# Second gate of the linear attention as a third seven-product block product, with two weight sums of each left to accumulating transfers

## The chip, the core and the metric

The kernel runs on one core of a Trainium2 chip. The time is device microseconds of one execution, the median of several; the profile is one more execution with the hardware profiler on. Engines are named as in the profile: PE is TensorE (PEld its weight loads), DVE is VectorE, ACT is ScalarE, POOL is GpSimd, SP is SyncE, which here only issues transfers.

## What is computed

One transformer block on 512 tokens of width 1024, in float32. A single weight `w_in` gives all projections of the normed input; two branches run from them, a gated linear attention in both directions with 4 heads and a latent attention with 8 heads; they are merged through two sigmoid gates, and a squared-ReLU network follows. What matters here, cut from the reference:

```python
n = rmsnorm(h, g_mix[l])
proj = n @ w_in[l]
(gq, gk, gv, gr, z_gf, z_gb, cq, ckv, kr, z_ma, z_mb) = jnp.split(proj, SPLIT_IDX, axis=-1)
...
o = rmsnorm(o_f + o_b, g_gla.reshape(GLA_HEADS, GLA_DV))
o = o.reshape(B, S, GLA_V_W) * jax.nn.silu(gr.astype(jnp.float32))     # y_gla
...
merged = jax.nn.sigmoid(z_ma) * y_gla + jax.nn.sigmoid(z_mb) * y_mla
h = h + merged @ w_out[l]
```

So the linear attention's output has two gates of the same width of 1024: the inner one, `gr`, and the outer one, `z_ma` (called za in the kernel). `z_mb` (zb) gates the latent attention.

## The kernel before, in words

**Precision.** Each float32 operand is split in a high part (rounded by a ScalarE copy, line 93) and a low part (the rest, by VectorE, line 94). `mm3` (lines 88 to 90) multiplies with three matmuls: high by high, high by low, low by high.

**Chunks.** A projection chunk is 128 columns of `w_in` against all 512 tokens: the weight (128x1024) is loaded by SP into one of 3 staging buffers, split into one of 4 pairs of weight buffers, and multiplied in 24 matmuls of 128x512 (`proj_begin`, `proj_run`). The result has features on partitions and tokens along the row. gq, gk, zb, za and the latents cq and ckv are done in such chunks. In za's case `za_gate` then multiplies by the row factor R on VectorE, takes tanh and a scale with bias (the gain of the norm) on ScalarE.

**Seven products.** gr and gv (1024 columns each) are done by class `Seven` as a 2 by 2 block product with seven multiplications instead of eight, after Winograd. Left factors are quarters of the input and four sums of them (`x_sums`, POOL); right factors are four weight blocks and four sums of them, made on VectorE (`less`, `right_sums`, line 608) in the place of a block. The order is 1, 2, 5, 6, 3, 7, 4. Each product is 24 matmuls of 128x512, and the results have tokens on partitions. Results of several products are added in six buffers c11, c12, c22 by ScalarE copies (line 660) and VectorE additions (line 663); a product that accumulates on an accumulator that was copied must wait for the copy. The sums and splits of a product are prepared two products ahead. Chunks are put between products as fillers: zb4, the small gate chunk, gq1, gk1 and, last, zb5.

**The heads.** For head h = 0 to 2 a loop gives PE, in this order: the scores (`gla_scores`: bd, then sc0 to sc3, with copies of bd on ScalarE and masked copies and splits on VectorE), the two gate matmuls of head h+1 (`Gates`), za chunk 2h, the output of head h (`gla_out`, 48 matmuls of 128x256), za chunk 2h+1, gq and gk of head h+2 (for head 2: ckv0, ckv1), and the eight transposes y of the gated output (`gla_turn`). Beside it run, for head h+1: logarithm, scans and exponentials of the gates (lines 442 to 479), the products q and k by decay on VectorE (`gla_qk`, line 489) and eight more on POOL (line 497); and for head h: squares on ScalarE, the norm on POOL (lines 717 to 719) and the gated rows on VectorE (`gla_gated`, line 727). POOL works in order, so the norm of head h stands behind the eight products of head h+1. After the transposes VectorE multiplies by the za gate (line 741).

**Head 3 and the step to the attention.** After the loop come cq0 to cq2, zb6, the scores of head 3, za6, the scaling of the query latent (cqrs), za7, the first part of zb7, the rotary query (ro, from the scaled and split latent cqhl), the rest of zb7, the first up-projections (uq0, uk0), the output of head 3, the values (uv), and then the first scores (s) of the latent attention. Chunks uq1 and uk1 come between its first scores. Calls of `goes_behind` and marks fix parts of that order on PE.

**What sets the order.** The program is written as one Python function under a tile scheduler, which places instructions on in-order queues, one per engine, and sets all waits. `in_program_order` fixes the written order for PE from the first product to the end of the heads, for ScalarE and VectorE from the start to the end of the heads, and for POOL through the block products; the rest the scheduler may order by its own costs. Tiles come from pools with a fixed number of buffers: 26 of 128x1024 (u4), 29 of 128x512 (u2), 4 and 4 PSUM banks (tags at and mm), and a tile whose pool is full waits until the last reader of an older one is done.

Of the kernel before, what the change touches and what calls it, by code (L numbers as in the profile page):

```python
# [18 lines left out]
P = 128  # L19
# [37 lines left out]
def tile_block(ctx: ExitStack, tc: tile.TileContext, t, out: bass.AP):  # L57
# [496 lines left out]

    SEVEN = (1, 2, 5, 6, 3, 7, 4)
# [35 lines left out]
    class Seven:  # L591
# [3 lines left out]

        def load(self, x):

            self.blocks[x] = [u4(f"{self.name}w{x}{g}", F32, (P, 2, S)) for g in range(2)]
            for g in range(2):
                r = ((x // 2) * 4 + 2 * g) * P  # L600
                c = self.col + (x % 2) * S
                nc.sync.dma_start(
                    self.blocks[x][g], w_in[r : r + 2 * P, c : c + S].rearrange("(k p) w -> p k w", p=P)
                )

        def less(self, dst, x, y):
            for g in range(2):
                nc.vector.tensor_tensor(
                    self.blocks[dst][g], self.blocks[x][g], self.blocks[y][g], op=ALU.subtract
                )  # L610
# [12 lines left out]
        def right_split(self, m, g):  # L623
            x = {1: 0, 2: 2, 5: 0, 6: 0, 3: 3, 7: 1, 4: 2}[m]
# [14 lines left out]
        def multiply(self, m):  # L639
# [18 lines left out]
            if m in (1, 5, 6):  # L658
                for acc, c in zip(accs, {1: self.c11, 5: self.c22, 6: self.c12}[m]):
                    nc.scalar.activation(c, acc, AF.Copy)  # L660
            elif m in (2, 3, 7):
                for acc, c in zip(accs, {2: self.c11, 3: self.c12, 7: self.c22}[m]):
                    nc.vector.tensor_tensor(c, acc, c, op=ALU.add)
# [22 lines left out]
    za_gates, held = {}, {}  # L686
# [42 lines left out]
    def gla_turn(h, early=None):  # L729
# [3 lines left out]
        for dv in range(2):  # L733
# [6 lines left out]
            y = za_gates.pop(f)  # L740
            nc.vector.tensor_tensor(y, tp, y, op=ALU.mult)
# [337 lines left out]
    sevens = [Seven(C_GR, "gr", gr_rows), Seven(C_GV, "gv", gv_rows)]  # L1079
# [6 lines left out]

    def begin_za(f):
# [581 lines left out]
```

## Time and profile before

| | |
|---|---|
| median of 3 runs | 763.39 us (763.17 to 763.4) |
| the profiled execution | 762.79 us |
| its span, first to last instruction | 761.0 us |
| mean granted clock of TensorE | 0.999 |
| DVE busy | 580.7 us, 76% of the span |
| ACT busy | 453.3 us, 60% |
| POOL busy | 150.5 us, 20% |

Line numbers such as L608 are those of the kernel before. A row of the timeline has start and length in us, engine, line, operation, output and inputs, the shape, how many instructions were merged (x2), and in brackets the idle time ahead of it with what ended that. A row of groups has the total busy time and the mean of one in ns. A row of transfers has the size of one and the median from issue to landing.

### The profile page before, as it was taken

The numbers are of one execution on the slowest core, as the hardware profiler recorded it, in microseconds if no ns is written. First come the engines' busy times: TensorE is split into PE (matmuls) and PEld (weight loads), VectorE is DVE, ScalarE is ACT, GpSimd is POOL, SyncE is SP. The second block draws the span as 40 slices with busy tenths as digits, with TensorE's granted clock in tenths as the row PEclk, the third lists the DMA queues.
The fourth block names the chain that finished last, engine by engine and source line by source line (L and its number), as shares of the span: only waits on it lengthen the run. The fifth ranks groups of instructions, "written<-read, shape, count | busy, mean of one in ns | idle before, by whom it ended". The sixth has DMA issues, their size and how long they took to land.

```text
span 761.0 us, 10233 instructions
## 1 busy us (share of the span) xinstructions
PE 752.1 (99%) x3744; PEld 636.1 (84%) x3744; DVE 580.7 (76%) x850; ACT 453.3 (60%) x768; POOL 150.5 (20%) x226
## 2 busy tenths in 40 slices
PE   9999999999999999999999999999999999999996
PEld 7888788888898889898888988888888888888885
DVE  7779999756767775998897786955796578748795
ACT  8456668475466555888866675435553555345644
POOL 0710005260615104127761100000000000000014
PEclk9999999999999999999999999999999999999999
DMA  9843310221324416127988421362116410650002
GB/s 312 255 112 108 93 28 28 56 59 54 84 60 112 82 33 155 25 71 191 272 189 229 140 80 56 111 196 80 55 56 195 137 42 15 195 165 1 28 1 110
DMA packets 97185, 81.28 MB, mean 107 GB/s; under 512 B 15504, under 2 KB 74896, under 8 KB 97136
## 3 DMA queue, kind: packets, MB, share of 16 engines
q1 hardware_dynamic: 93904, 74.33, 33.3%
q0 software_dynamic: 2944, 6.03, 4.3%
q8 instruction: 29, 0.48, 0.3%
q10 hardware_dynamic: 288, 0.28, 0.1%
q14 instruction: 20, 0.16, 0.1%
HBM read 76.96 MB, written 2.10 MB: 104 GB/s over the span
## 4 chain that ended last, share of the span: by engine, by line
PE 97%; DVE 1%; ACT 1%; issue 0%; POOL 0%; POOLq 0%; ACTq 0%
PE f L88 8%; PE f L89 8%; PE f L90 8%; PE gx L88 4%; PE gx L90 4%; PE gx L89 4%; PE first L327 3%; PE tp L1042 2%; PE za L88 2%; PE za L89 2%; PE za L90 2%; PE gz L88 2%; PE gz L90 2%; PE gz L89 2%; PE zb L88 1%; PE zb L90 1%
## 5 line engine op out<-in xcount | busy, mean ns | idle before, releaser
L1608 POOL DMA_DIRECT2D gfin<-in_g_final x1 | 0.6, 622 | 284.0 <-PE f L90 284.0
L914 DVE TENSOR_TENSOR w<-w,w 128x1024 f32<-128x1024 f32 x32 | 38.7, 1221 | 0.3
L475 POOL COPY v3f<-rrf 128x4 f32<-128x4 f32 x4 | 2.8, 708 | 135.9 <-DVE rrf L458 135.9
L1027 ACT ACTIVATE e<-s,top 128x512 f32<-128x512 f32 x32 | 21.9, 685 | 4.8 <-DVE top L1022 3.9
L94 DVE TENSOR_TENSOR pT<-tp,pT 128x512 fp32r<-128x512 f32 x32 | 21.7, 682 | 2.9 <-ACT pT L93 2.9
L1022 DVE TENSOR_REDUCE top<-s 128x1 f32<-128x512 f32 x32 | 21.6, 681 | 2.0 <-PE s L90 1.7
L1335 DVE TENSOR_TENSOR h<-h,gx 128x512 f32<-128x512 f32 x32 | 21.5, 682 | 1.9 <-PE gx L90 1.8
L93 ACT ACTIVATE pT<-tp 128x512 fp32r<-128x512 f32 x32 | 18.8, 593 | 4.2 <-PE tp L1042 3.9
L1042 PE MATMUL tp<-ident,e 128*128 128x128 f32 x128 | 19.3, 274 | 0.4 <-ACT e L1033 0.2
L88 PE MATMUL av<-pT,v 128*128 128x256 f32 x64 | 19.0, 297 | 0.0
L93 ACT ACTIVATE ghb<-y 128x512 fp32r<-128x512 f32 x16 | 10.1, 632 | 14.0 <-DVE y L860 14.0
L1401 ACT ACTIVATE fa<-f 128x512 f32<-128x512 f32 x32 | 18.5, 577 | 0.0
L89 PE MATMUL av<-pT,v 128*128 128x256 f32 x64 | 18.2, 285 | 0.0
L1042 PEld LDWEIGHTS tp<-ident,e 128*128 128x128 f32 x128 | 15.1, 140 | 3.7 <-ACT e L1033 1.0
L94 DVE TENSOR_TENSOR sc<-sc,sc 128x512 fp32r<-128x512 f32 x16 | 10.9, 691 | 9.5 <-ACT sc L93 9.5
L90 PE MATMUL av<-pT,v 128*128 128x256 f32 x64 | 18.1, 283 | 0.0
L93 ACT ACTIVATE sc<-sc 128x512 fp32r<-128x512 f32 x16 | 9.3, 596 | 11.5 <-DVE sc L546 11.5
L93 ACT ACTIVATE b_00h<-w 128x1024 fp32r<-128x1024 f32 x7 | 7.4, 1061 | 12.6 <-PE gx L90 6.0
L93 ACT ACTIVATE b_20h<-w 128x1024 fp32r<-128x1024 f32 x7 | 7.4, 1061 | 12.1 <-PE gx L90 6.0
L93 ACT ACTIVATE b_10h<-w 128x1024 fp32r<-128x1024 f32 x7 | 7.4, 1061 | 12.1 <-PE gx L90 6.0
L88 PE MATMUL s<-kbuf,q 96*128 96x512 f32 x32 | 14.1, 440 | 0.0
L1410 ACT ACTIVATE px<-fa 128x256 f32<-128x256 f32 x32 | 13.4, 418 | 1.0
(1667 smaller groups left out, 2927.9 us busy)
## 6 DMA issues: line engine op xcount, KB each, us to landing
w<-in_w_ff SPq DMA_DIRECT2D x64, 256.0 KB, 3.5
w<-in_w_out POOLq DMA_DIRECT2D x10, 512.0 KB, 9.4
grw<-in_w_in SPq DMA_DIRECT2D x8, 512.0 KB, 8.5
gvw<-in_w_in SPq DMA_DIRECT2D x8, 512.0 KB, 4.6
w<-in_w_out SPq DMA_DIRECT2D x16, 256.0 KB, 5.8
x<-in_xt SPq DMA_DIRECT2D x8, 256.0 KB, 5.2
vw<-in_w_first SPq DMA_DIRECT2D x8, 256.0 KB, 5.3
h<-in_x SPq DMA_DIRECT2D x4, 512.0 KB, 5.0
```

The source lines that it names most:

```text
L88: nc.tensor.matmul(acc, lh, rh, start=start, stop=False, skip_group_check=onto)
L89: nc.tensor.matmul(acc, lh, rl, start=False, stop=False, skip_group_check=onto)
L90: nc.tensor.matmul(acc, ll, rh, start=False, stop=stop, skip_group_check=onto)
L93: nc.scalar.activation(hi, src, AF.Copy)
L94: rest.tensor_tensor(lo, src, raw(hi), op=ALU.subtract)
L327: nc.tensor.matmul(f_accs[i], a[:, i * P : (i + 1) * P], b, start=k == 0 and x == 0, stop=k == KD - 1 and x == 2)
L914: nc.vector.tensor_tensor(wq[dst][g], wq[x][g], wq[y][g], op=op)
L1022: nc.vector.tensor_reduce(top, acc, axis=AX.X, op=ALU.max, negate=True)
L1027: nc.scalar.activation(e, acc, AF.Exp, bias=top, accum_out=tot[:, qt % 2 : qt % 2 + 1])
L1042: nc.tensor.transpose(tp[:, k * P : (k + 1) * P], e[:, k * P : (k + 1) * P], ident)
L1335: nc.vector.tensor_tensor(hc, hc, acc, op=op)
L1401: nc.scalar.activation(a, acc, AF.Relu)
```

## The change

The za projection leaves the chunks and becomes a third `Seven` between gr and gv. Its result has tokens on partitions, as the gated rows of gr have, and `za_rows` multiplies (tanh + 1) into the rows `g1` at once; `za_gate` is gone. At the end of a head ScalarE scales the transposed rows by the norm's gain (line 736 after) where VectorE multiplied by the gate before.

In `Seven` the signs of the left sums are turned, so that two of the four weight sums become plain additions of a block of `w_in` onto a block that is there already. These two are issued by POOL as accumulating transfers of 512 KB (`onto`, twice two per weight), after the splits of product 5 and of product 6; VectorE keeps the other two sums.

The places of the za chunks are filled otherwise: zb5 moves from ahead of the first scores into head 0, zb6 into head 1, ckv0 into head 2, ckv1 and cq0 behind its output; `gla_qk` of head 0 comes ahead of product 7 of gv; the step from head 3 to the attention is written in a new order (scores of head 3, cq1, cq2, its output, zb7, cqrs and directly the rotary query). In the built program uq1 and uk1 then stand ahead of the first score of the latent attention.

```diff
-            add(y[:, LO], a[:, HI], b[:, HI], op=ALU.add)
+            add(y[:, LO], a[:, HI], b[:, HI], op=ALU.subtract)
...
-            add(z[:, HI], b[:, LO], x_y[p][:, HI], op=ALU.subtract)
+            add(z[:, HI], b[:, LO], x_y[p][:, HI], op=ALU.add)
...
-        def less(self, dst, x, y):
+        def onto(self, dst, x):
+
             for g in range(2):
-                nc.vector.tensor_tensor(
-                    self.blocks[dst][g], self.blocks[x][g], self.blocks[y][g], op=ALU.subtract
-                )
+                nc.gpsimd.dma_start(self.blocks[dst][g], self.source(x, g), accum_op=ALU.add)
 
         def right_sums(self, m):
-            if m == 5:
-                self.less(0, 1, 0)
-            elif m == 6:
-                self.less(0, 3, 0)
-            elif m == 3:
-                self.less(2, 2, 0)
-            elif m == 7:
-                self.less(1, 3, 1)
+            if m in (5, 6):
+                for a, b in zip(self.blocks[0], self.blocks[1 if m == 5 else 3]):
+                    nc.vector.tensor_tensor(a, a, b, op=ALU.add)
             self.right[m] = []
...
             for g in range(2):
                 self.right_split(m, g)
+            if m == 5:
+                self.onto(1, 3)
+            elif m == 6:
+                self.onto(0, 2)
...
-                    nc.scalar.activation(c, acc, AF.Copy)
+                    nc.scalar.activation(c, acc, AF.Copy, scale=-1.0 if m == 6 else 1.0)
...
-                    nc.vector.tensor_tensor(c, acc, c, op=ALU.add)
+                    nc.vector.tensor_tensor(c, c, acc, op=ALU.subtract if m == 7 else ALU.add)
...
-    def za_gate(f, acc):
-
-        z = u2(f"za{f}")
-        nc.vector.tensor_tensor(z, acc, R, op=ALU.mult)
-        nc.scalar.activation(z, z, AF.Tanh, scale=0.5)
-        gain = gla_gain[:, f : f + 1]
-        nc.scalar.activation(z, z, AF.Identity, bias=gain, scale=gain)
-        za_gates[f] = z
+    def za_rows(i, half, src, dst):
+
+        nc.scalar.activation(dst, src, AF.Tanh, scale=r_half[:, i : i + 1])
+        g = g1[i, half]
+        nc.vector.scalar_tensor_tensor(g, dst, 1.0, g, op0=ALU.add, op1=ALU.mult)
...
-            y = za_gates.pop(f)
-            nc.vector.tensor_tensor(y, tp, y, op=ALU.mult)
+            y = u2(f"yg{f}")
+            nc.scalar.activation(y, tp, AF.Copy, scale=gla_gain[:, f : f + 1])
...
-    sevens = [Seven(C_GR, "gr", gr_rows), Seven(C_GV, "gv", gv_rows)]
+    sevens = [Seven(C_GR, "gr", gr_rows), Seven(C_ZA, "za", za_rows), Seven(C_GV, "gv", gv_rows)]
...
-        w_b = begin_za(2 * h + 1)
-        acc = proj_run(w_a, xT)
         if h < 2:
-            w_a, lows = begin_late(C_GQ + (h + 2) * P, f"gq{h + 2}")
+            acc = proj_run(w_a, xT)
+            w_b, lows = begin_late(C_GQ + (h + 2) * P, f"gq{h + 2}")
         else:
-            ckv_.begun[0], lows = begin_late(C_CKV, "ckv0")
+            ckv_.run(0)
+            ckv_.begun[1], lows = begin_late(C_CKV + P, "ckv1")
...
-        za_gate(2 * h, acc)
+        if h < 2:
+            g2.append(gated(acc, f"b{5 + h}")[1])
...
-        za_gate(2 * h + 1, proj_run(w_b, xT))
...
-    cq_.run(0)
-    marks.append(traced())
...
+    sc = gla_scores(near, nxt, far)
+    in_turn()
     ckv_.sums()
+    cq_.run(1)
+    in_turn()
+    cq_.begin(2)
+    cq_.run(2)
+    in_turn()
+    os = gla_out(h, sc)
+    in_turn()
...
+    g2.append(gated(proj_T(C_ZB + 7 * P, "zb7"), "b7")[1])
+    in_turn()
+    rs = gla_squares(h, os)
+    gla_gated(h, os, rs)
     cq = cq_.normed()
-    za_gate(7, proj_T(C_ZA + 7 * P, "za7"))
     kbuf = rotary_k()
...
     ro = rotary_q()
```

More of the change, by code (lines that the diff above doesn't have):

```diff
@@ L1103, in tile_block @@
         (0, 6): (lambda: z_chunk_begin("mm"), z_chunk_run),
-        (1, 2): (lambda: begin_qk(1, 0), lambda w: finish_qk(1, 0, w)),
+        (2, 2): (lambda: begin_qk(1, 0), lambda w: finish_qk(1, 0, w)),
     }
-    steps = [(a, m) for a in range(2) for m in SEVEN]
+    steps = [(a, m) for a in range(3) for m in SEVEN]
     ordered = traced()
@@ L1114, in tile_block @@
         ahead = steps[n + 2]
-        if a == 0:
-            for x in {3: (0,), 7: (2, 1), 4: (3,)}.get(m, ()):
-                sevens[1].load(x)
+        if a < 2:
+            for x in {5: (0,), 6: (2,), 7: (1,), 4: (3,)}.get(m, ()):
+                sevens[a + 1].load(x)
         if steps[n + 1] in fillers:
@@ L1164, in tile_block @@
     gv.multiply(3)
+    near, nxt, far = gla_qk(0, gate.parts)
     gv.multiply(7)
-    near, nxt, far = gla_qk(0, gate.parts)
     gv.right_split(4, 1)
-    w_b = begin(C_ZB + 5 * P, "zb5")
     gv.sinks(3)
@@ L1171, in tile_block @@
     finish_qk(1, 1, w_k)
+    w_a = begin(C_ZB + 5 * P, "zb5")
     gv.product(4)
-    w_a = begin_za(0)
-    finish_zb(5, w_b)
     ckv_, cq_ = Latent(C_CKV, 2, V_KV, "ckv"), Latent(C_CQ, 3, V_Q, "cq")
@@ L1194, in tile_block @@
         rs = gla_squares(h, os)
-        za_gate(2 * h + 1, proj_run(w_b, xT))
         if h < 2:
-            w_b = begin_qk(h + 2, 1)
+            w_k = begin_qk(h + 2, 1)
             gla_gated(h, os, rs)
-            finish_qk(h + 2, 0, w_a)
-            w_a = begin_za(2 * h + 2)
-            finish_qk(h + 2, 1, w_b)
+            finish_qk(h + 2, 0, w_b)
+            if h == 0:
+                w_a = begin(C_ZB + 6 * P, "zb6")
+            else:
+                ckv_.begin(0)
+            finish_qk(h + 2, 1, w_k)
         else:
-            ckv_.begin(1)
+            cq_.begin(0)
             gla_gated(h, os, rs)
-            ckv_.run(0)
-            cq_.begin(0)
             ckv_.run(1)
+            cq_.begin(1)
+            cq_.run(0)
         gla_turn(h)
```

55 lines of the change are left out of this document (13 added, 42 removed).

## The prediction

> **What bounds the kernel now.** I read the page's head and chain first, then who waits on TensorE, then the timeline by engine around the linear attention. In the page, see that PE is busy for the whole span and carries nearly all of the chain; in the waits of PE, that in 761 us it waited only at the start and once, 0.4 us, for VectorE.
>
> ```profile
> span 761.0 us, 10233 instructions
> PE 752.1 (99%) x3744; PEld 636.1 (84%) x3744; DVE 580.7 (76%) x850; ACT 453.3 (60%) x768; POOL 150.5 (20%) x226
> PE 97%; DVE 1%; ACT 1%; issue 0%; POOL 0%; POOLq 0%; ACTq 0%
> ...
> PE warm L317 <- POOL ident masks.py:199: 1.5, 1, 1.5
> PE grx L88 <- DVE grc L663: 0.4, 1, 0.4
> ```
>
> So any work taken from TensorE is worth its full time, as long as the other engines keep up with a PE that arrives earlier. That is the question here, for the gate chunks za0 to za7 that the change takes away stood between dependent steps, as cover.
>
> **TensorE work.** The start times show what a chunk costs:
>
> ```profile
> 146.90 0.39 PE L88 MATMUL za<-xT,za0h 128*128 128x512 f32 x1
> 152.34 0.28 PE L88 MATMUL gla0o<-gv,sc 128*128 128x256 f32 x1
> ```
>
> 24 matmuls take 152.34 - 146.90 = 5.44 us. A block product is 24 matmuls of that shape too. Eight chunks become seven products: -5.44 us. The built order of the changed program agrees: 3,503 rows on PE for 3,527. Everything else on PE only moves: za now runs (38.1 us) ahead of the value projection, and zb5, zb6, zb7 and the latent chunks take some of the places that za0 to za7 had.
>
> **The block-product stage.** Products follow each other without a gap, but from product 7 to product 4 of one weight the accumulators have to be read first:
>
> ```profile
> 76.92 1.23 DVE L94 TENSOR_TENSOR gr41l<-grw,gr41h 128x1024 fp32r<-128x1024 f32 x1 [0.83 <-ACT gr41h L93]
> 80.77 1.28 DVE L663 TENSOR_TENSOR grc<-grx,grc 128x512 f32<-128x512 f32 x2
> 81.60 0.47 PE L88 MATMUL grx<-gr40h,xT 128*128 128x512 f32 x1 [0.42 <-DVE grc L663]
> ```
>
> The split gr41 waits for product 3 to free its weight buffer, and the sums and gates behind it on VectorE fill the whole of product 7, so the read of grx comes late. The order of za is the same: I add the same price once more, 0.4 us by the row, 0.7 us with the slow start behind it. The value projection has a chunk there, as before.
>
> Dropping two sums on VectorE per weight (16 instructions become 12) against 6 more splits, 6 more accumulator reads and 8 gate multiplications fewer leaves VectorE with as much as before (826 rows for 827; ScalarE has 12 more), and the stage that holds the additions is 38 us longer on PE: I cost it at nothing. The accumulating transfers have their price in these rows:
>
> ```profile
> w<-in_w_out POOLq DMA_DIRECT2D x10, 512.0 KB, 9.4
> gvw<-in_w_in SPq DMA_DIRECT2D x8, 512.0 KB, 4.6
> 105.73 1.22 DVE L94 TENSOR_TENSOR gv61l<-gvw,gv61h 128x1024 fp32r<-128x1024 f32 x1
> 122.46 1.05 ACT L93 ACTIVATE gv40h<-gvw 128x1024 fp32r<-128x1024 f32 x1
> ```
>
> One lands 9.4 us after issue (below: 4.6, as a plain load; above: twice 9.4, if the pair queue up). It can start when split 6 has read the block (107.0) and is read by split 4 at 122.5, 15.5 us later: hidden at 9.4, and about 3 us late at the top, most of which the lead of the split over its product takes. I take nothing, and keep 0 to +6 us for three weights. Behind these issues on POOL stand two memsets and the small copies of the first gates, due many us later. That an accumulator copy carries a scale of -1 I take as free: the copy forms with a scale already run here.
>
> **The heads: the chain that loses its cover.** For head 0, with times from its first score (bd):
>
> ```profile
> 142.03 0.38 PE L528 MATMUL bd<-qkb 128*128 128x128 f32 x2
> 153.34 1.06 ACT L450 ACTIVATE l<-l 128x1024 f32<-128x1024 f32 x1
> 155.38 1.22 DVE L94 TENSOR_TENSOR za1l<-za1f,za1h 128x1024 fp32r<-128x1024 f32 x1 [3.56 <-ACT za1h L93]
> 156.52 1.36 DVE L458 TENSOR_TENSOR_SCAN rrf<-mf,l 128x128 f32<-128x128 f32 x4
> 169.96 0.61 POOL L497 TENSOR_TENSOR qk<-qkb,c3b 128x256 f32<-128x256 f32 x1
> 172.06 0.20 POOL L719 TENSOR_TENSOR gla0ss<-gla0ss,r_x 128x4 f32<-128x4 f32 x1
> 173.09 0.87 DVE L727 SCALAR_TENSOR_TENSOR grd<-gla0o,gla0ss,grd 128x256 f32<-128x256 f32 x2
> 174.73 0.38 PE L737 MATMUL y<-ident,gra 128*128 128x128 f32 x2
> 175.60 0.61 PE L528 MATMUL bd<-qkb 128*128 128x128 f32 x4
> ```
>
> See a second path beside PE's: scores, splits, gate logarithm (ends 154.40), scans, exponentials, eight products on POOL, the row norm behind them on POOL (172.26), the gated rows on VectorE (end 173.96), and only then the transposes y that PE has ahead of the next head's bd. From bd to the gated rows are 31.9 us; PE arrived at y after 32.7. The margin is 0.8 us.
>
> The change takes one chunk of 5.4 us out of PE's path to y: it arrives at 27.3. From the other path it takes only the split za1l ahead of the scan: the scan can start at 154.45 for 156.52, 2.1 us earlier. What stands behind it (scans, POOL, norm, rows) is unchanged in the built order. The gated rows are there at 29.9 us, five of the eight transposes follow at 0.11 us, and the next bd is at 30.4 instead of 33.6 (175.60 - 142.03). Without the wait it would be at 28.1. So a head gains 3.15 us instead of 5.44: **the wait gives back 2.3 us per head**, part of it at gk2, whose split comes later than PE too. Heads 1 and 2 have the same queues: three times 2.3 = +7.0 us.
>
> **The tail, head 3 to the attention.** Here za6, za7, half of zb7 and zb6 stood as cover.
>
> ```profile
> 244.50 0.49 DVE L792 TENSOR_SCALAR ang<-ang,gvec 128x512 f32<-128x512 f32 x1
> 248.76 1.42 DVE L797 SCALAR_TENSOR_TENSOR ang<-turns,ang 128x512 f32<-128x512 f32 x2
> 253.81 0.72 ACT L804 ACTIVATE cos<-turns,half_pi 128x512 f32<-128x512 f32 x1 [0.69 <-DVE turns L802]
> 276.35 0.62 PE L298 MATMUL cqrs<-cqdg,ones_r 128*128 128x512 f32 x2
> 278.66 1.66 ACT L93 ACTIVATE cqhl<-cqc 128x512 fp32r<-128x512 f32 x3
> 279.42 1.89 DVE L94 TENSOR_TENSOR cqhl<-cqc,cqhl 128x512 fp32r<-128x512 f32 x3
> 284.31 0.39 PE L88 MATMUL ro<-cqhl,wr0h 128*128 128x512 f32 x1
> 298.26 0.38 ACT L716 ACTIVATE gla3sq<-gla3o 128x256 f32<-128x256 f32 x1 [0.23 <-PE gla3o L90]
> 303.82 0.40 PE L88 MATMUL s<-kbuf,q 96*128 96x512 f32 x1
> 310.42 0.66 PE L1042 MATMUL tp<-ident,e 128*128 128x128 f32 x4 [0.25 <-ACT e L1033]
> ```
>
> Three waits arise, by the built order.
> First, the copy of bd stands on ScalarE behind sine and cosine, and these wait for VectorE, where three splits (1.2 us each) and the angle (some eight instructions of 0.5 to 0.7 us) come only after the gated rows. That ends about 9.6 us after bd, the copy at 10.2; PE wants the bank for the last scores at 8.4 (3.4 for bd and three of the four scores, 5.0 for 22 matmuls of cq1). About +1.9 us (bounds 0 and 4).
> Second, the query latent: before, its scaling (cqrs, 276.35) had 8.0 us of other matmuls until ro. Now ro stands right behind it, with 1.4 us of cover (uk0). The first high half needs a multiplication and its turn on ScalarE, behind a tanh and four squares (4 x 0.36): 3.0 us. The low halves stand on VectorE behind the gated rows of head 3, which wait for ScalarE and POOL: another 1.3 us. Together +4.3 us (bounds 2 and 6).
> Third, from the first attention score to the first transpose of it were 6.6 us, and PE had scores and the chunks uq1 and uk1 for all of that. These two now run ahead of the scores. The latency stays near 5.5 us, the four scores fill 2.7: +2.8 us (bounds 1 and 4).
> These make 9.0. I take 8.1 of them: the 0.25 us in the last row goes, and the first of the three is the least sure.
>
> **The sum**: -5.44 + 0.7 + 7.0 + 8.1 = +10.4 us. The profiled execution took 762.79 us (span 761.0 and 1.8 around it), so 773.2, and I say **773.0**. The median of the runs shown, 763.39, is 0.6 above the profiled one, inside what I can claim.
>
> **Rivals.**
> Covered after all (faster): the tile scheduler's order lets every wait fall on work that is ready, and only -5.44 counts: 757.4. For it: VectorE and ScalarE are busy only 76% and 60%. Against it: the queues are in order and the chain above is latency, not load; it decides where the gated rows are there 27.3 us after bd, 2.6 us before my 29.9. Chance 0.09.
> Only the heads wait, the tail is covered: -5.44 + 0.7 + 7.0 = +2.3, 765.1. For it: my tail is put together from many short rows. Chance 0.12.
> Late transfers: the accumulating pairs hold split 4 or 7 up, +6 on top: 779. Against it: 15.5 us of room. Chance 0.04.
> The clock: waits of TensorE could lower its granted clock.
>
> ```profile
> 754.17 0.28 PE L90 MATMUL gend<-b_31h,ga 128*128 128x256 f32 x1
> 755.00:758.00 3.00, 0.00 (x0) 0.00 (x0) 1.48 (x3) 1.84 (x4) 0.55 (x1) 1.00 0.88 324
> 758.00:761.00 3.00, 0.00 (x0) 0.00 (x0) 0.00 (x0) 0.00 (x0) 0.00 (x0) 0.66 0.47 175
> ```
>
> These windows (PEclk is the third number from the right) show it at 1.00 for 3.6 us after the last matmul and falling within the next 3, to a mean of 0.66. My longest wait is 3.0 us, but two stand close at ro. If it fell there and at each head, and half speed held for as long as the idle row shows, each of four or five drops would cost about 2 us: +9, 782. Chance 0.06. [...]
> That the change does not do what it says is excluded by the 24 matmuls that are gone from PE's queue.
>
> **Chances and range.** Forecast 0.69 (766.5 to 777.5), the rivals as above. Faster by over 0.2% (1.5 us, about what a measurement of this kernel can tell from no change): 0.10; within: 0.05, the lower edge of the covered tail; slower: 0.85. For 8 in 10 the range takes in the forecast's own and the covered tail, and goes up to the late transfers: 763.5 to 779.
>
> **What would show it.** In the profile after: PE's share of the chain falls, and waits of PE appear by name: y on the gated rows (L722) and gk2, gk3, cq0 on their splits, some 2.5 us a head, with bd to bd at about 30.4; sc3 behind the copy of bd; ro behind cqhl, 4 us; tp behind e, 2.8 us. za products follow each other without a wait but one of 0.4 us at product 4, and no split waits for an accumulating transfer. If bd to bd is 28 us, the chain through POOL is wrong and the gain stays. If the waits are there and the time is still lower, the tail was.

## The result and the profile after

The changed kernel takes **779.65 us** (median of 4) where the one before takes 763.39: a ratio of 1.0226, 95% interval 1.0201 to 1.0251, so it is slower, by more than forecast (773.0) and just above the range (779). The four executions took 779.42 to 784.15 us, those of the kernel before 763.17 to 763.41. The profiled execution took 779.85 us, with a span of 778.1, 17.1 more than before. TensorE's mean granted clock is 0.992, before 0.999.

From the page of the kernel after, the head, the busy time of the engines and the chain that ended last:

```profile
span 778.1 us, 10266 instructions
PE 754.5 (97%) x3720; PEld 633.9 (81%) x3720; DVE 584.3 (75%) x850; ACT 463.1 (60%) x780; POOL 162.6 (21%) x238
PE 77%; DVE 8%; ACT 8%; POOL 4%; issue 2%; DMA 0%; SPq 0%; POOLq 0%; DVEq 0%; ACTq 0%
```

PE's share of the chain fell from 97% to 77%, and VectorE, ScalarE and POOL have 20%: for a good part of the time the bound is a chain through them. 24 matmuls are gone, yet PE is busy 2.4 us longer; part of that is half clock, as shown below. The waits of PE by name (line waited on and its releaser; total us, times, longest):

```profile
PE ro L88 <- ACT cqhl L93: 4.4, 1, 4.4
PE tp L1037 <- ACT e L1028: 2.8, 1, 2.8
PE sc L540 <- ACT bds L532: 1.6, 1, 1.6
PE warm L317 <- POOL ident masks.py:199: 1.5, 1, 1.5
PE uk L88 <- DVE q L98: 1.5, 1, 1.5
PE cq L88 <- ACT cq0h L93: 1.3, 1, 1.3
PE y L732 <- DVE gra L722: 0.5, 2, 0.3
PE gk L90 <- DVE gk2l L94: 0.5, 1, 0.5
PE cq L90 <- DVE cq0l L94: 0.5, 1, 0.5
PE gk L90 <- DVE gk3l L94: 0.5, 1, 0.5
PE grx L88 <- DVE grc L663: 0.4, 1, 0.4
PE zax L88 <- DVE zac L663: 0.4, 1, 0.4
```

Two rows of 0.3 and 0.2 us are left out. Before, this view had the `warm` and the `grx` row and one of 0.2 us at tp. Where in the span they lie, from PE's timeline of the kernel after, the first score of each head and the places of the longer waits:

```profile
175.21 1.05 PE L528 MATMUL bd<-qkb 128*128 128x128 f32 x8
...
205.77 1.06 PE L528 MATMUL bd<-qkb 128*128 128x128 f32 x8
...
236.16 1.06 PE L528 MATMUL bd<-qkb 128*128 128x128 f32 x8
...
268.06 1.06 PE L528 MATMUL bd<-qkb 128*128 128x128 f32 x8
...
278.39 0.49 PE L540 MATMUL sc<-qkf 128*128 128x128 f32 x2 [1.63 <-ACT bds L532]
...
304.05 0.80 PE L88 MATMUL ro<-cqhl,wr0h 128*128 128x512 f32 x1 [4.45 <-ACT cqhl L93]
...
320.33 0.47 PE L88 MATMUL uk<-ckvhl,wk1h 128*128 128x512 f32 x1 [1.51 <-DVE q L98]
...
327.49 0.66 PE L1037 MATMUL tp<-ident,e 128*128 128x128 f32 x4 [2.80 <-ACT e L1028]
```

The first transpose of the attention starts at 327.49, before at 310.42: 17.07 us later, which is the whole difference of the spans. Behind it nothing differs. So the stage that got longer lies between the block products and that row, and it lost 17.07 + 5.44 = 22.5 us in waits and slow clock. Three parts:

| part | forecast | measured | how |
|---|---|---|---|
| block products | 0.7 | 0.5 | head 0's first score 33.2 later; the products less zb5 give 32.7 |
| heads 0, 1, 2 | 7.0 | 9.0 | 30.56, 30.39, 31.90 from bd to bd; without a wait 28.1, 28.0, 27.8 |
| head 3 to the attention | 8.1 | 13.0 | the rest |

The four longer waits are 10.4 of the 13.0 in the last row. Most of what is missing there, and part of the heads', is the clock. Windows of the kernel after (length, busy time of PE, PEld, DVE, ACT and POOL with counts; the third number from the right is the granted clock):

```profile
257.28:260.70 3.42, 1.59 (x6) 0.73 (x5) 1.23 (x1) 3.42 (x10) 3.42 (x8) 1.00 0.01 2
298.28:301.69 3.41, 1.32 (x6) 0.75 (x4) 2.68 (x5) 2.72 (x6) 2.25 (x4) 1.00 0.01 2
301.69:305.10 3.41, 1.05 (x3) 0.86 (x4) 1.16 (x2) 3.34 (x12) 1.38 (x3) 0.50 0.31 58
305.10:308.52 3.42, 3.42 (x10) 2.65 (x9) 3.36 (x7) 0.23 (x1) 0.03 (x1) 0.50 0.00 0
325.58:329.00 3.42, 1.51 (x13) 1.51 (x14) 2.90 (x7) 3.15 (x7) 0.00 (x0) 1.00 0.96 295
```

Around cq0 and ro the clock was 0.50, for 3.4 us from 260.70 and for 6.8 us from 301.69. The 8 and some 10 matmuls in them start 0.43 us apart instead of 0.227: 1.6 and 2.0 us. The forecast had put nothing there.

The accumulating transfers, the part that costs nothing, in the list of transfers of the kernel after (count, size, median us from issue to landing):

```profile
grw<-in_w_in POOLq DMA_DIRECT2D x4, 512.0 KB, 8.7
zaw<-in_w_in POOLq DMA_DIRECT2D x4, 512.0 KB, 6.7
gvw<-in_w_in POOLq DMA_DIRECT2D x4, 512.0 KB, 6.7
```

8.7 and 6.7 us, under the 9.4 that the forecast took, and no row of the waits of PE, VectorE or ScalarE names them.

### The profile page after: what moved, and what is told of

It is laid out like the page before. It is cut to its first block, busy times and chain, and to the rows that moved or that the text cites. A ratio compares the mean times of both kernels' runs of the same rounds, so it can differ in the third digit from the quotient of the medians.

```text
span 778.1 us, 10266 instructions
## 1 busy us (share of the span) xinstructions
PE 754.5 (97%) x3720; PEld 633.9 (81%) x3720; DVE 584.3 (75%) x850; ACT 463.1 (60%) x780; POOL 162.6 (21%) x238
## 4 chain that ended last, share of the span: by engine, by line
PE 77%; DVE 8%; ACT 8%; POOL 4%; issue 2%; DMA 0%; SPq 0%; POOLq 0%; DVEq 0%; ACTq 0%
PE f L89 7%; PE f L90 7%; PE f L88 7%; PE gx L88 4%; PE gx L89 4%; PE gx L90 4%; PE first L327 3%; POOL qk L497 2%; PE gz L88 2%; PE gz L89 2%; PE gz L90 2%; PE tp L1037 2%; PE av L89 1%; PE av L90 1%; PE av L88 1%
## 5 line engine op out<-in xcount | busy, mean ns | idle before, releaser
L1068 POOL TENSOR_TENSOR mx<-tb,yg 128x256 f32<-128x256 f32 x8 | 7.4, 919 | 37.0 <-DVE tot L1027 23.5
```

## The experiments

**The theories.** Mine: the forecast's chains are right, and what it missed is the clock and a wait further on in the tail; so a chain that is shortened, or a clock that is kept up, gives its time back. The rival: behind each wait stands the next one, since VectorE, ScalarE and POOL have the same work in the same order whatever PE does; then single repairs gain little, and only an order that gives PE other work at every dependent step gains. Each kernel below differs from the kernel after, but for the ninth, which differs from the kernel before. Stretches are read from the timelines of the profiled executions: from the first score of head 0 to that of head 3 (heads), and from there to the first transpose of the attention (tail).

| run | heads | tail | median us | ratio to before, 95% |
|---|---|---|---|---|
| after | 92.9 | 59.4 | 779.65 | 1.0226 [1.0201, 1.0251] |
| 1 idle matmuls | 91.2 | 63.2 | 782.51 | 1.0250 [1.0235, 1.0265] |
| 2 splits earlier | 91.1 | 65.7 | 784.41 | 1.0276 [1.0260, 1.0292] |
| 3 norm earlier | 87.1 | 59.8 | 775.89 | 1.0165 [1.0148, 1.0182] |
| 4 both | 85.7 | 65.5 | 780.71 | 1.0234 [1.0219, 1.0250] |
| 5 angle later | 91.3 | 61.9 | 780.28 | 1.0220 [1.0201, 1.0239] |
| 6 = 4 + 5 | 85.7 | 64.0 | 776.87 | 1.0176 [1.0161, 1.0191] |
| 7 tail covered | 91.3 | 59.8 | 780.12 | 1.0215 [1.0199, 1.0230] |
| 8 = 4 + 7 | 85.7 | 61.4 | 775.50 | 1.0153 [1.0138, 1.0168] |
| 9 before, transfers alone | | 43.9 | 763.19 | 1.0001 [0.9992, 1.0009] |
| 10 sums by VectorE | 91.3 | 63.2 | 789.37 | 1.0329 [1.0303, 1.0355] |
| 11 refilled | 96.5 | 50.5 | 776.16 | 1.0165 [1.0151, 1.0179] |
| 12 refilled, cq later | 85.7 | 51.8 | 766.68 | 1.0041 [1.0029, 1.0054] |
| 13 rows of head 3 later | 91.3 | 63.8 | 783.81 | 1.0288 [1.0266, 1.0311] |
| 14 = 12, angle in heads | 88.7 | 50.1 | 768.25 | 1.0059 [1.0045, 1.0072] |
| 15 = 12, angle later | 85.7 | 57.2 | 769.80 | 1.0075 [1.0061, 1.0089] |
| 16 = 12, angle in gv | 86.8 | 52.1 | 767.97 | 1.0055 [1.0041, 1.0068] |
| 17 = 12, angle in gr and za | 85.7 | 45.3 | **761.35** | **0.9974 [0.9964, 0.9985]** |

In 9 the heads hold the za chunks, so that stretch doesn't compare. Before, the tail took 43.9. Heads and tail are of one execution each; where the half clock falls in it moves them by some us, as runs 1 and 10 show.

### 1. Is it the clock?

The kernel after with 5 more matmuls of 128x512 ahead of cq0 and 18 ahead of ro, into a bank that nobody reads, only to keep PE busy:

```diff
+    def idle_matmuls(n, name):
+        acc = ps("at", name)
+        for _ in range(n):
+            nc.tensor.matmul(acc, ones_r, xT[0][:, 0, :], start=True, stop=True)
...
+            idle_matmuls(5, "idle0")
...
+    idle_matmuls(18, "idle1")
```

> The changed kernel with 5 matmuls that nobody reads between ckv1 and cq0 and 18 between cqrs and ro, in places where TensorE stood idle; all other instructions as they were. Theory (the clock): the granted clock falls to 0.5 twice, behind the waits at cq0 (8 matmuls of 0.43 us for 0.23) and at ro (10 of 0.43), and that costs 1.6 + 2.0 us on top of the waits. With TensorE kept busy the clock stays at 1.00, the waits on ScalarE end at the same time, and the kernel takes 776.0 us for 779.65. Rival (waits only): the matmuls at half clock only fill time in which TensorE would have waited again, at y and at uk1 on VectorE: 779.6, as before.

782.51 us: not faster, rather slower. The two drops are gone, and the heads are 1.7 us shorter, but others come at 278, 322 and 329: three stretches of 3.4 us at half clock, together as much as in the kernel after. From the waits of PE in this run:

```profile
PE sc L540 <- ACT bds L532: 3.1, 1, 3.1
```

The wait for the copy of bd took up what cq0 gave: 3.1 instead of 1.6 us, and the score behind it starts at 278.37, in the kernel after at 278.39. From cqrs to the first attention score are 22.76 us, after 22.82. So those moments are set on the other engines; at these two places PE at half clock was only filling time in which it would have waited. For them my first theory fell. Run 10 below bears it out from another side. Its program is the same behind the block products, but by chance the clock stays up at cq0: its heads take 91.3 us instead of 92.9, and sc3 waits 3.0 us instead of 1.6.

That doesn't make half clock free. Between bd of head 3 and cqrs PE has matmuls back to back but for the wait at sc3, and a drop there costs its full price. In the kernel after this stretch has none and takes 30.9 us. Run 1 takes 33.8: 1.5 more by the longer wait, 1.4 by the drop at 278. Run 10 takes 35.3: 1.4 by the wait and 3.0 by 6.8 us of half clock from 285.2. So a longer wait at sc3 is paid twice, and that, with the drops at 322 and 329, is why run 1 is slower than the kernel after.

### 2, 3, 4. The heads

Run 2 makes the splits of gk2, gk3 and cq0 earlier, between the exponentials. Run 3 puts the norm of head h (POOL) between the two halves of the eight POOL products of head h+1, instead of behind them. Run 4 does both.

```diff
+            w_k, lows = begin_late(C_GK + (h + 2) * P, f"gk{h + 2}")     # runs 2 and 4
...
-        near, nxt, far = gla_qk(h + 1, gate.parts)
-        rs = gla_squares(h, os)
+        near, nxt, far, rs = gla_qk(h + 1, gate.parts, lambda: gla_squares(h, os))     # 3 and 4
```

> The changed kernel with the splits of gk2, gk3 and cq0 issued on ScalarE before the squares of the output and not behind them. Theory (two paths that end together): in heads 0 and 1 the waits at gk2 and gk3 go (0.8 and 0.5 us by name, 1.4 and 1.4 with the slow starts behind them), but the gated rows come no earlier, so the wait at y takes their place: no gain there. In head 2 the wait of 1.83 us at cq0 and the half clock behind it go and a wait at y of about 1.5 us comes: 1.6 us less. 778.0. Rival (waits add up): each wait is worth its own length: 1.4 + 1.4 + 1.9 + 1.6 less, 773.4.

> The changed kernel with the row norm of head h on POOL placed in the middle of the eight products of head h + 1, four products ahead of it and four behind, and not behind all eight. Theory: the gated rows are there about 3 us earlier, so the wait at y goes (0.9 us each in heads 0 and 1), and gk2, gk3, cq0 wait as they do: 1.8 less, 777.9; the last products end 1 us later and just meet the first scores. Rival: the products end too late and the scores wait for POOL: 779.6 or more, with a wait of sc on qk.

> Both edits together: splits of gk2, gk3, cq0 ahead of the squares, the norm between the products on POOL. Theory: both paths of a head are shortened, and bd to bd falls from 30.56, 30.39 and 31.90 us to what TensorE's own work takes, 28.1, 28.0 and 27.8: 2.4 + 2.4 + 4.1 = 8.9 less than 779.65, 770.8. Rival (the scores wait next, for the products on POOL that now end last): only half of that, 775.

In run 2 the waits of gk and cq are gone, and y waits 1.5, 1.5 and 1.3 us instead: heads 0 and 1 gain nothing (30.49 and 30.33 from bd to bd). In run 3 the y waits are gone and a head takes 29.2. So the POOL chain was the bound, as the prediction had it, with the splits second. With both, run 4, a head takes 28.7, 28.7 and 28.3, where 28.1, 28.0 and 27.8 is PE's own work: 7.2 us less than after, 1.6 of them the clock at cq0. None of it arrives. The longest waits of PE in run 4:

```profile
PE ro L88 <- ACT cqhl L93: 4.4, 1, 4.4
PE sc L546 <- ACT bds L538: 4.2, 1, 4.2
```

sc3 waits 4.2 us for 1.6, and the clock is then at 0.50 for 10.2 us, from 273.7 to 283.9. The stretch from bd of head 3 to cqrs, first in the kernel after and then in run 4 (columns as in the windows above):

```profile
268.06:298.97 30.91, 29.28 (x172) 25.48 (x171) 19.36 (x42) 11.76 (x22) 3.03 (x3) 1.00 0.30 51
261.83:299.40 37.57, 33.41 (x172) 29.03 (x171) 21.22 (x43) 12.54 (x23) 4.54 (x4) 0.86 0.24 42
```

It is 6.7 us longer: 2.5 by the wait, and 4.1 because the same 172 matmuls keep PE busy for 33.41 us instead of 29.28. So of what the heads gave, more went into half clock behind the wait than into the wait itself. The median is 780.71, as after. Run 3 won less in the heads and kept most of it (775.89), with a wait of 2.5 us there and the clock at 1.00 from 258 to 290. None of the four expectations gave the time: runs 1, 2 and 4 came out slower than both of their numbers, run 3 faster than both.

### 5 to 8. The tail

What holds the copy of bd up, from the timeline of ScalarE in the kernel after:

```profile
272.28 0.53 ACT L93 ACTIVATE wr0h<-wr0f 128x384 fp32r<-128x384 f32 x1 [2.50 <-DMA wr0f<-in_w_uq]
...
276.41 0.63 ACT L798 ACTIVATE sin<-ang 128x512 f32<-128x512 f32 x1 [2.30 <-DVE ang L794]
277.13 0.72 ACT L799 ACTIVATE cos<-turns,half_pi 128x512 f32<-128x512 f32 x1
277.76 0.58 ACT L532 ACTIVATE bds<-bd 128x512 f32<-128x512 f32 x1
```

The copy (`bds`) stands behind sine and cosine and these behind the angle on VectorE, as forecast. VectorE itself was held up inside the angle by the low split of wr0, 1.6 us, because that weight's load came late; this was not in the forecast. Run 5 takes the angle, sine and cosine behind the scores of head 3; run 6 adds the heads of run 4; run 7 is run 5 with the query latent, ro and the output of head 3 spread apart, the gated rows of head 3 behind ro, and uq1, uk1 between the attention scores again; run 8 is run 7 with the heads of run 4.

```diff
-    cos, sin = rotary_tables()
     marks = [traced()]
...
     sc = gla_scores(near, nxt, far)
+    cos, sin = rotary_tables()        # 5 to 8
     in_turn()
...
             next(units, None)
+            if n in (2, 3):           # 7 and 8
+                goes_behind((upped, traced()), scored, PE_ONLY)
```

> The changed kernel with the sine and cosine tables written behind the scores of head 3 and not ahead of them, so that the copy of bd stands ahead of sine and cosine on ScalarE and all scores of head 3 follow bd directly. Theory: the wait of 1.6 us at the last scores goes with its slow start, 1.7 us less: 777.9. Rival (a fixed later wait takes it up, as the three runs before showed for gains made further ahead): 779.6, with a wait at cq2, ckvrs or ro that is longer by as much.

> The kernel of the run e4 (splits early, norm between the products) with the tables behind the scores too. Theory: in e4 the heads gained 7.2 us from bd of head 0 to bd of head 3 (85.7 for 92.9 us), and all of it was given back at one place, the copy of bd behind sine and cosine, whose wait grew from 1.6 to 4.2 us and brought a drop of the granted clock with it. With that copy ahead of sine and cosine the gain stays: 779.65 - 7.2 - 1.7 = 770.7. Rival (the next wait of the tail takes it): 775 or more.

> The changed kernel with the heads as they are and the tail rewritten: tables behind the scores; three eighths of zb7 ahead of cqss, the output of head 3 between cqss and cqrs, the other five eighths of zb7 between cqrs and ro; squares, norm and gated rows of head 3 behind the rotary query; uq1 and uk1 behind the first scores of the attention. Theory: the waits of the tail are cover that was lost, sc3 1.7, ro 4.4 with 2.0 of half clock behind it, uk1 1.5, tp 2.8: 12.4 less than 779.65, 767.3. Rival (VectorE and ScalarE bound the tail, whatever TensorE's order): 773 or more.

> Heads of e4 and the tail of e7 together. Theory: the two gains add, 7.2 and 12.4 less than 779.65: 760.0, which is faster than the kernel before (763.4) by about what the missing chunk is worth less 2 us. Rival (the covered work is longer than TensorE's): between 762 and 767.

Each wait that was aimed at went away, and another came. In run 5 sc3 no longer waits, ckvss does (2.8 us, released by VectorE's split of the scores), and 3.4 us of half clock follow at 275.5, still ahead of cqrs: 780.28. In runs 7 and 8 ro and uk don't wait any more, and tp only 0.3 us. The longest waits of PE in run 8:

```profile
PE s L88 <- DMA q<-ro: 5.8, 1, 5.8
PE ckvss L269 <- DVE sc L94: 2.9, 1, 2.9
```

The first attention score waits for the transfer that brings the rotated query to its place, and the clock is at 0.50 for 10.2 us from 309.4. The rival's number held in runs 5, 6 and 7; run 8, at 775.50, is above both of its numbers. Run 8 is 4 us faster than the kernel after, but by the heads: these are 7.2 us shorter, its tail 2.0 longer.

### 9, 10. The accumulating transfers

Run 9 is the kernel before with the new signs and the accumulating transfers, and nothing else of the change. Run 10 is the kernel after with the two sums on VectorE, at the same places:

```diff
-                nc.gpsimd.dma_start(self.blocks[dst][g], self.source(x, g), accum_op=ALU.add)
+                nc.vector.tensor_tensor(self.blocks[dst][g], self.blocks[dst][g], self.blocks[x][g], op=ALU.add)
```

> The kernel before (two block products, za in chunks) with the signs of the sums turned and two of the four weight sums of each product made by accumulating transfers. Theory: the transfers are hidden behind TensorE, which the 76% busy VectorE doesn't limit: 763.4, no difference. Rival (the transfers or the lighter VectorE matter): up to 4 us more (pairs that land late), or 1 us less (the read of the accumulators ahead of product 4 comes sooner).

> The changed kernel with all four weight sums of each block product on VectorE again, no accumulating transfers. Theory: the transfers cost nothing and gain nothing: 779.65. Rival: each of three products waits longer ahead of product 4, because VectorE has 2.5 us more per sum: 1 to 6 us more; or the transfers were the cost: 1 to 6 us less.

Run 9: 763.19, ratio 1.0001 [0.9992, 1.0009]: the transfers by themselves neither cost nor bring anything. For run 10 I expected no difference either; it is 9.7 us slower than the kernel after, and 6.1 of them are there at the first score of head 0 (181.32 for 175.21); behind that the program is the same, and the other 3.6 go back to where the clock falls, as said under run 1. The window of za's products in run 10, and its wait:

```profile
91.00:116.00 25.00, 22.41 (x95) 17.88 (x94) 23.88 (x25) 13.76 (x19) 0.00 (x0) 0.97 0.22 65
```

```profile
PE zaz L88 <- ACT zac L660: 2.2, 1, 2.2
```

and the same window of the kernel after:

```profile
91.00:116.00 25.00, 25.00 (x112) 20.72 (x111) 20.75 (x22) 15.26 (x20) 4.84 (x4) 1.00 0.87 210
```

With the sums VectorE (third pair) is busy 23.9 of 25.0 us and PE has gaps; without them 20.8, and PE has none. gr and gv have chunks between their products, which give VectorE time; za has none. So with all four sums VectorE bounds a block product without fillers, and the transfers are what makes room for the third one: without them it would cost some 6 us more.

### 11 to 17. Cover put back

If the rival is right, the loss belongs to the order and not to the block product. Run 11 gives the heads and the tail other cover: cq0, cq1, cq2 in heads 0, 1 and 2 (where zb5, zb6 and ckv0 stand), zb5, zb6 and zb7 between the dependent steps of the tail, ckv0 and ckv1 behind the output of head 2, with run 4's splits and norm, and uq1, uk1 between the attention scores. Run 12 moves the copy, square and sum of each cq chunk on ScalarE and VectorE behind the splits, and the scaling of the key latent behind ro. Run 13 is a single edit to the kernel after, for the wait at ro.

```diff
-            acc = proj_run(w_a, xT)                    # 11, 12
+        acc = proj_run(cq_.begun.pop(h), xT)
...
+            lows()
+            cq_.keep(h, acc)                           # 12: here, in 11 ahead of lows()
...
+    g2.append(gated(proj_run(w_a, xT), "b5")[1])       # 11, 12: in the tail
...
-    rs = gla_squares(h, os)                            # 13: from ahead of normed()
-    gla_gated(h, os, rs)                               #     to behind rotary_q()
```

> The changed kernel with other chunks in the places that za left: cq0, cq1, cq2 in heads 0 to 2, ckv0 and ckv1 behind the output of head 2, and zb5, zb6, zb7, on which nothing waits, in the tail: scores of head 3, zb5, cqrs, zb6, ro, zb7, uq0, uk0, output of head 3, uv, first scores; splits and norm in the heads as in e4, uq1 and uk1 behind the first scores. Theory (the chunks for cover were spent in the heads, where a chunk of the latents would have done, and were missing in the tail, where a chain of dependent steps runs): all waits of the tail go, about 1.5 us of splits stays in the heads: 759.5, faster than the kernel before by the missing chunk less those. Rival (the tail's chain is longer than any order of TensorE covers): 766 or more, with waits at ro, s or tp.

> The kernel of e11 with two changes: the copy, square and sum of a cq chunk stand behind the split of gk3 and ckv1 on ScalarE and VectorE and not ahead of them, and the scaling of the key latent (ckvrs) stands behind the rotary query. Theory: e11 lost 3.9 us at gk3 and 3.9 at ckv1 with half clock behind each, because VectorE waited for the square ahead of those splits, and 1.7 at ckvrs with half clock at ro; without them bd to bd is 28.7 us in all heads, and the kernel takes 761, faster than the kernel before. Rival (the tail's chain from cqrs to the first score, some 22 us in every kernel here, decides): 766 or more.

> The changed kernel with only the squares, norm and gated rows of head 3 written behind the rotary query, so that on ScalarE four squares and on VectorE the gated rows no longer stand between cqrs and the splits of the query latent; uq1 then falls behind the first scores by itself. Theory: what decides behind cqrs is not the wait at ro but the whole chain through ScalarE and VectorE to the first score, 22.8 us with the clock at half and 22.8 with it kept up (e1); it falls by about 2.7 us, and uq1 covers the wait at tp: 775. Rival (the wait at ro is set by the splits of the weights ahead of it on ScalarE): ro 1 us earlier, 778.5.

Run 11 takes 776.16: the tail is 8.9 us shorter, but gk3 and ckv1 wait 3.9 us each, since VectorE stood 3.3 us ahead of their splits, waiting for ScalarE's square of a cq chunk, and half clock follows each. Run 12 undoes that: 766.68, heads 28.3, 28.3 and 29.1. The longest of PE's waits that are left:

```profile
PE zb L88 <- DVE ckvc L776: 2.4, 1, 2.4
...
PE uk L89 <- DVE ckvhl L94: 1.1, 1, 1.1
```

In run 13 ro waits 3.0 instead of 4.4 us, but VectorE then comes late with kbuf, an up-projection waits 5.9 us for it, and the time is 783.81. From cqrs to the first attention score are now 23.3 us instead of 22.8. That one edit tells no more of these than that VectorE's order matters in them.

What seemed to hold run 12 was the angle, eight instructions of VectorE in the tail. Run 14 puts it into heads 0 and 1 (and the rotary query behind the key latent again), run 15 behind the scaling of the key latent, run 16 in one piece into gv's block product, run 17 in four pieces ahead of splits in gr and za. Run 17 also has SP issue the rotated queries of the first two heads ahead of other transfers, and the rotary key later.

```diff
+                if g == 0 and m in (7, 4) and self.name != "gv":     # 17, in right_split
+                    next(angle)
...
+        if (a, m) == (2, 2):                                         # 16, in the block products
+            cos, sin = rotary_tables(nc.vector)
...
+    goes_behind((at, traced()), rotated, SP_ONLY)                    # 17
```

> The kernel of e12 with the chain of the rotary angle on VectorE (eight instructions, some 5 us) and sine and cosine on ScalarE taken from the tail and put into heads 0 and 1, where VectorE waits 3 us for the gated rows; ckrs of the key latent stands ahead of the rotary query again. Theory (what is left in the tail is VectorE's queue): e12 still lost 6.6 us between bd of head 3 and the first transpose of the attention (51.8 us for 45.2 of TensorE's own), 2.4 at zb7 and 1.1 at uk behind the angle, with half clock behind the first; without the angle these go, 5 us less than 766.7: 761.5, faster than the kernel before. Rival (the angle only moves the wait into head 1, to the gated rows): 766.

> The kernel of e12 with the rotary angle left in the tail, but written behind the scaling of the key latent, so that on VectorE the gate of zb6 and the scaling stand ahead of the angle and give their accumulators back early. Theory: in e12 zb7 waited 2.4 us for an accumulator that VectorE held behind three steps of the angle, with half clock of 3 us behind it, and uk 1.1; these go, and with them 4 to 5 us: 762. Rival (the rotated query comes later by as much, and the first score waits for it): 766.7 or more.

> The kernel of e12 with the angle on VectorE and sine and cosine on ScalarE moved into the block products of gv, between product 2 and the chunk gq1, where a chunk gives TensorE cover of 5.4 us. Theory: the tail falls from 51.8 us to about 47.5 (e12's wait at zb7, the half clock behind it and most of the wait at uk go), the block products take the 5 us of VectorE without a wait of TensorE: 762.5, equal to the kernel before or just under it. Rival (VectorE, busy 83% in that stage, is the bound there): products of gv wait, by up to 5 us: 767.

> The kernel of e16 with the angle cut into four groups of one to two instructions, each between two splits of products 7 and 4 of gr and za, where VectorE waits 1.5 us for ScalarE; and with the four small transfers of the rotated query of heads 0 and 1 issued ahead of the transfers of the key buffers and of the prefetches for w_out, which stood before them in SP's queue. Theory: e16 lost 2.6 us to VectorE in the block products and 3.7 at the first score to transfers that were issued 8 us after their data were there, with 2 us of half clock behind; without both: 760.5, faster than the kernel before. Rival (the next wait of the tail takes it): 766.

Runs 14 and 15 show the rival once more: 3.0 us longer heads in the first, and in the second uk waits 3.6 us for the rotation and the first attention score 3.1 for a transfer. Run 16 is at its rival's number, but in the main for another wait: the first attention score waits 3.7 us for the transfer of the rotated query. SP's own queue in run 16 shows where that stood:

```profile
296.81 0.80 SPq L923 DMA_DIRECT2D bo11f<-in_w_out  x2
297.72 1.84 SPq L847 DMA_DIRECT2D kbuf<-kbuf  x3
299.67 6.69 SPq L988 DMA_DIRECT2D q<-ro  x8
```

The first score needs the first two of the eight. They are issued at 299.67 and 300.24, behind the weight loads and three copies of the key, and land late besides. From issue to landing (shortest, median, longest), the first two of run 16 and then the first four of run 17, where they are issued ahead of those transfers:

```profile
DMA to landing us min/median/max: 6.2/6.4/6.5
DMA to landing us min/median/max: 2.3/2.3/2.3
```

Run 17 takes both edits, the angle in pieces and the order on SP. Its tail is 6.9 us shorter than run 16's, about what the wait of 3.7 us and the 6.8 us at half clock behind it cost there; so that part goes with the order of the transfers (the run doesn't separate it from the rotary key, which comes later too). Its page and its waits of PE, which are four:

```profile
span 759.5 us, 10266 instructions
...
PE 82%; DVE 9%; ACT 6%; issue 1%; POOL 1%; POOLq 0%; DVEq 0%; ACTq 0%
```

```profile
PE zax L88 <- DVE zac L671: 1.7, 1, 1.7
PE warm L317 <- POOL ident masks.py:199: 1.5, 1, 1.5
PE uv L88 <- DVE q L98: 1.1, 1, 1.1
PE grx L88 <- DVE grc L671: 0.4, 1, 0.4
```

761.35 us, ratio 0.9974 [0.9964, 0.9985]: the third block product with its transfers, in another order, is faster than the kernel before. It gains 2.1 us, where the matmuls that are gone are worth 5.44; the pieces of the angle cost about 1.3 us at the block products, where zax waits 1.7 us for 0.4.

## Why the prediction was wrong in size

**Right.** TensorE's work: 24 matmuls are gone. The block products: 0.5 us against 0.7, with the wait at zax 0.4, as named. The transfers at nothing: shown by run 9. The heads' chain through POOL: bd to bd 30.56 and 30.39, forecast 30.4; that it is POOL's eight products with the norm behind them, and the splits second, is shown by runs 2, 3 and 4. The three waits of the tail, each at its place and by its releaser: sc3 1.6 (forecast 1.9), ro 4.4 (4.3), tp 2.8 (2.8). No rival was right: covered after all, only the heads and late transfers didn't come; the clock did fall, twice, but run 1 shows that these two drops set nothing in the kernel after.

**Wrong.** The failed steps are two terms of the sum. The tail, "These make 9.0. I take 8.1 of them", was 13.0. Most of what is missing is in its second item, the query latent, "Together +4.3 us": it was priced as far as ro and taken for done there. The stretch from cqrs to the first attention score in the kernel after:

```profile
298.97:321.79 22.82, 16.87 (x76) 13.61 (x75) 18.49 (x30) 15.07 (x37) 10.61 (x17) 0.85 0.29 60
```

PE is busy for 16.87 of 22.82 us, and 2.0 of these are half clock. So 8.0 us are lost where the forecast had 4.3: the wait at ro, 4.4, a fourth wait, uk1 for VectorE's split of the query, 1.5, and the half clock. With 1.6 at sc3 and 2.8 at tp that is 12.4; short rows are the rest. "Heads 1 and 2 have the same queues: three times 2.3" was 2.4, 2.4 and 4.1: behind head 2 stands cq0, with two waits of 1.3 and 0.5 us and 1.6 of half clock. What these terms share: I counted PE's waits against PE's work, one by one. From cqrs on this isn't what decides: in the kernel after and in runs 1 to 6, 10 and 13 that stretch takes 22.2 to 23.3 us, whether the clock falls in it or not. It is set by a chain on the other engines, VectorE and ScalarE by the waits above and SP by those of runs 7 and 8, and I hadn't added it up to its end. Ahead of cqrs a wait taken away came back too, in runs 2, 4 and 5, but there as a wait together with half clock behind it. In the profile of before the material was there: the splits on VectorE, the scalings and copies on ScalarE, eight transfers of the rotated query on SP. One thing wasn't there: ahead of sc3, the load of wr0, late by 1.6 us for VectorE. And one reading was short, at no cost to the sum: before, PE waited a third time, 0.2 us at tp, the row that the third item uses.

**The clock rival.** I had let it need 3.6 us of idle time. It fell 2.1 us after PE's last matmul ahead of ro, and at cq0 after waits of 1.3 and 0.5 us, as below. Its price adds to the others in some places only: at cq0 the next wait grew by as much when the clock stayed up (1.6 to 3.1), and at ro nothing changed behind it, but between bd of head 3 and cqrs each drop cost its full price (runs 1, 4 and 10).

**Open.** Which single instruction of VectorE sets the 22.8 us from cqrs to the first score in the kernel after: run 13 moved two of its items and met a third. What an order with the full clock in front of cqrs would give to the heads of run 4; the idle matmuls of run 1 only moved the drops. And whether the kernel before would gain from run 17's order of VectorE and SP without the third block product; this wasn't tried.

## What to carry to other kernels

Work that is taken from the engine that bounds the kernel may have been the cover of a chain elsewhere: list, per dependent step, how long the chain on the other engines is, and how much of the bounding engine's work lies beside it before and after. A wait found in that way isn't a term by itself; if the chain goes on behind it, add up the chain to its end, or the repair of one wait pays for the next. Where the bounding engine is TensorE and its own work decides, a wait can also bring half clock behind it, and then costs more than its length: in run 4, 2.5 us more of waiting at sc3 came with 4.1 us of half clock behind it. Put back cover in the shape of independent work at every dependent step, and move short work of a full engine to a stage where it has room, before judging the saving itself.

## What the runs showed of the hardware

**The clock fell after less idle time than the forecast took.** In the kernel after it fell to 0.50 at 301.69, 2.1 us after PE's last matmul, and at 260.70 after two waits of 1.3 and 0.5 us with two matmuls between. It stayed there for 6.8 and 3.4 us; of the other stretches at 0.50 named above, that of run 5 took 3.4 us, those of runs 10 and 16 6.8 and those of runs 4 and 8 10.2. In the 3.4 us ahead of the two falls PE was busy for 1.32 and 1.59 us. That measure alone doesn't tell: from 325.58 to 329.00, in the fence of windows above, PE was busy for 1.51 of 3.42 us, and the clock was 1.00 there and up to 332.40. Work on PE didn't bring the full clock back at once: in run 4 PE was busy for all of 276 to 282 us, and the clock was 0.50 all that time and until 283.9. And the same two waits at cq0, 1.3 and 0.5 us, came with 1.6 us of half clock in the kernel after and with none in runs 5, 7, 10 and 13 (heads of 92.9 and 91.3); what decides between the two was not shown.

**A transfer of 64 KB kept SP for 0.51 to 0.58 us, and landed later behind others.** That is what each of the eight issues of the rotated query took in the kernel before. In run 16 the first two of them are 0.57 us apart, and the eight take 6.69 us from first to last, waits between them included. Issued behind seven other transfers, the first two landed 6.2 and 6.5 us after issue; in run 17, issued ahead of them, 2.3 us after. So the urgent transfer was better issued first.
